# A mixed change to a tuned encoder layer: weight splits moved to VectorE, a norm moved to another buffer, row picks moved ahead of a weight split

## The chip, the core and the metric

The kernel runs on one core of a Trainium2 chip. The metric is the device time of one execution in microseconds (us). Matrix products run on TensorE (PE in the profile, its weight loads PEld), elementwise work on VectorE (DVE), activations and copies on ScalarE (ACT), and further elementwise work, indexed gathers and accumulating scatters on GpSimd (POOL). SyncE (SP) issues the plain transfers. Each engine takes its instructions in the order of its own queue; between engines semaphores hold them back.

## What is computed

One encoder layer, for 2048 sample tokens and 512 prompt tokens with the same weights, in float32:

```
h = x + W_out @ concat[DiffAttn(n), BandGQA(n)],  n = RMSNorm(x)
y = h + ExpertChoiceSwiGLU(RMSNorm(h))

def expert_choice_ffn(x, w_router, w_gate, w_up, w_down):     # once for each group
    C = CAPACITY_FACTOR * T // N_EXPERTS                       # 256 sample rows, 64 prompt rows
    aff = jax.nn.softmax(jnp.dot(xt, w_router), axis=-1)
    gates, idx = lax.top_k(aff.T, C)                           # each of 16 experts takes its C best tokens
    xe = xt[idx]
    h = jax.nn.silu(einsum('ecd,edf->ecf', xe, w_gate)) * einsum('ecd,edf->ecf', xe, w_up)
    ye = einsum('ecf,efd->ecd', h, w_down) * gates[..., None]
    y = zeros.at[idx].add(ye)
```

The model width is 1024 and each expert's inner width 1024.

## The kernel before, in words

Tokens are worked on in 20 blocks of 128 (b = 0 to 19; 16 of the sample, `NS`, and 4 of the prompt, `NP`; `NB` is 20). A float32 product is made of three faster ones (`mm3`, L167 to L169): each operand is split into a high part (a copy that rounds, on ScalarE) and a low part (the difference, on VectorE or GpSimd).

The stage that matters first is the loop over blocks that makes the output projection (`outproj`), adds the residual (L1409), and makes the second norm (`norm2`): ScalarE squares and sums a row into `dst`, GpSimd takes the power -1/2, and the norm `n2` is written (by VectorE at L1424, or, for blocks that `slow` names, by ScalarE and GpSimd) and stored to DRAM (`n2s_d` for the sample, `n2p_d` for the prompt). One block later the norm is transposed and split (`split_n`), multiplied with the router's weights (`router`, L1433) and turned into affinities (`router_2`: softmax; `router_3`: transposed copy for the search).

Work of one block is woven into the products of another by hand: `at(t, f, ...)` books a function for tick t of the current block, and `tick` is called after each product of eight. A generator does the top-k: `choose` finds each expert's threshold by ten steps of three bits. A step counts on VectorE (`flags`, L1204), asks TensorE for a sum over the candidates (L1212), and reads the answer (`r`, L1213). Each `yield` ends a slot. `first_sample` runs the sample's search over the last blocks' ticks (`SLOTS`), then writes the one-hot selections of expert 0 (`onehot_s`, L1308) and picks its rows.

`pick` turns one-hot selections into row numbers: small products on TensorE (L1329), a copy `ax` and `idx` and `gate` on VectorE (L1332 to L1334), then gathers on GpSimd (L1342), two of 128 sample rows and one of prompt rows.

After the last block `last_block`, another generator, makes the router of block 19, and, woven into expert 0's first product, the prompt's search and the picks for experts 0 and 1. Expert 0's first turns (`first_turn`, L1570) transpose the gathered rows.

The experts follow one after another. The first product (`gate_up`) goes over eight chunks f of the inner width; after half of a chunk it calls `mid`, which books the split of a later chunk's weights (`w_split`), loads (`w_load`) and, in certain chunks, the next expert's one-hots (f = 0) and pick, and from f = 4 on the transposes of the next expert's rows (`turn`, L1584). Experts 2 to 15 make the second product in blocks (`down_blocks`) and end with scatters (L1810) that add the rows to the output: `x.ys[1]`, the two halves of the prompt's `x.ys[2]` (both write `out_p`, so that the second waits until the first has landed), and `x.ys[0]`.

Weights of 1 MB a chunk are loaded into a ring of two `wraw` buffers, and every third early one into the room of `affsT` (the sample's transposed affinities, no longer needed once the search is over). In expert 0, `w_split` works by quarters of 512 columns: the high part on ScalarE (L1292) and the low part on GpSimd (L1293).

Of the kernel before, what the change touches and what calls it, by code (L numbers as in the profile page):

```python
# [8 lines left out]
F32 = mybir.dt.float32  # L9
# [9 lines left out]
P = 128  # L19
D = 1024  # L20
# [6 lines left out]
E = 16  # L27
# [80 lines left out]
def hybrid_encoder_kernel(tc, a, out_s, out_p):  # L108
# [11 lines left out]
    with ctx:  # L120
# [33 lines left out]
        def pow_mhalf(out, in_, n):  # L154
            nc.gpsimd.tensor_tensor(out, in_, nhalf[:, :n], op=OP.pow)
# [19 lines left out]
        with ExitStack() as st:  # L175
# [521 lines left out]
            def at(dt, f, *args):  # L697
                events.append((clock[0] + dt, len(events), f, args))
# [579 lines left out]
                raws.append((key, raw))  # L1278
                loaded[0] += 1

        def w_split(part=None):

            if raws:
                key, raw = raws[0]
                if not part:
                    split[key] = [wsp.tile([P, 2048], F32R, name=f"w{c}") for c in ("hi", "lo")]
                hi, lo = split[key]
                if part is None:
                    split_w(hi, lo, raw)
                else:  # L1290
                    cs = slice(part * 512, (part + 1) * 512)
                    nc.scalar.activation(hi[:, cs], raw[:, cs], AF.Copy)  # L1292
                    nc.gpsimd.tensor_sub(lo[:, cs], raw[:, cs], hi[:, cs].bitcast(F32))  # L1293
                if part is None or part == 3:
                    raws.pop(0)

# [63 lines left out]
        with ExitStack() as st:  # L1360
# [24 lines left out]
            def slow(b):  # L1385
                return NS <= b < NB - 1
# [21 lines left out]
                h = H[b]  # L1408
                nc.vector.tensor_add(h[:, cs], o, h[:, cs])  # L1409

            def norm2(b):
                out, n2d, r, aff = where(b)
                h = H[b]
                nc.sync.dma_start(out[r * P:(r + 1) * P, :], h)
                s = wk.tile([P, 3], F32, name="dst")
                n2 = tk.tile([P, D], F32, name="n2")
                nc.scalar.activation(n2, h, AF.Square, accum_out=s[:, 0:1])
                nc.vector.tensor_scalar(s[:, 1:2], s[:, 0:1], 1.0 / D, EPS, op0=OP.mult, op1=OP.add)
                pow_mhalf(s[:, 2:3], s[:, 1:2], 1)
                if slow(b):  # L1420
                    nc.scalar.activation(n2, h, AF.Copy, scale=s[:, 2:3])
                    nc.gpsimd.tensor_mul(n2, n2, ffn_g)
                else:
                    nc.vector.scalar_tensor_tensor(n2, h, s[:, 2:3], ffn_g, op0=OP.mult, op1=OP.mult)  # L1424
                nc.sync.dma_start(n2d[r * P:(r + 1) * P, :], n2)
                N2[b] = n2
# [40 lines left out]
                    split_wo_l(1, h, k, nc.vector)  # L1467
            split_w(wrh[:, :, 0, :], wrh[:, :, 1, :], wrr)

            SLOTS = (2, 7, 12, 17), (4, 9, 14), (1, 6, 11, 14, 16, 17)  # L1470
            gens = []

            def slot():
# [9 lines left out]
            for b in range(NB):  # L1483
                if b + 2 < NB:
                    MX[b + 2] = load_mx(b + 2)
                if b + 1 < NB:
                    load_res(b + 1)
                if b == 0:
                    for j in range(HEADS * NP):
                        at(14 + 18 * j, lambda j=j: Prompt(0, j // NP, j % NP).start())  # L1490
                    for h in range(2, HEADS):
                        at(72 * h - 50, load_prompt, h)
                if b == NS + 1:
                    rest.close()
                    wsp = pool(ctx, "wsE", 3, side="right")
                if b >= 1:
                    if slow(b - 1):
                        at(12, split_n, b - 1)
                    t = 15 if slow(b - 1) else 13
                    at(t, router, b - 1)  # L1500
                    at(t + 2, router_2, b - 1)
                    if b < NS:
                        at(t + 7, router_3, b - 1)
                    if b == NS:
                        gens.append(first_sample(X[0]))
                        parts = gate_parts(affs, auxs, NS, "s")
                        at(17, router_3, b - 1)
                        at(17, slot)
                if b > NS:
                    at(1, router_3, b - 2) if b > NS + 1 else None  # L1510
                    for t in SLOTS[b - NS - 1]:
                        at(t, slot)
                    at(9, next, parts, None)
                    at(14, next, parts, None)
                if b == 2:
                    at(3, places, auxs, NS)
                    at(9, places, auxp, NP)
                if NS < b < NB - 1:
                    for i in range(4):
                        at(1 + 4 * i, w_split, i)  # L1520
                if b == 0:
                    tick(8)
                else:
                    outproj(b, 0)
                if b >= 1 and not slow(b - 1):
                    split_n(b - 1)
                tick(1)
                if b + 1 < NB:
                    MT[b + 1] = split_m(MX[b + 1])
                tick(1)  # L1530
                outproj(b, 1)
                norm2(b)
                if b == 1:
                    w_load()
                    w_load()
            while gens:
                slot()

        stay.close()

# [6 lines left out]
        with ExitStack() as st:  # L1547
# [123 lines left out]
            def down_blocks(x):  # L1671
# [69 lines left out]
                p = bank("gu1")  # L1741
                product(p, 5, "22b")
                added(y[2][1], q, 2, y[2][1])
                scatter_p(x, x.ys[2])
                added(y[0][1], p, 0, y[0][1])
                scatter(x.idx[:, 0:1], x.ys[0], out_s)
                w_split()
                w_load()

# [64 lines left out]
                for gi in range(2):  # L1814
                    scatter(x.idx[:, gi:gi + 1], x.ys[gi], out_s)

            def scatter_p(x, y):
                for hf in range(2):
                    scatter(x.idx[:CP, 2:3], y[hf * CP:(hf + 1) * CP, :], out_p)

            def last_block(x, y):
# [55 lines left out]
            for f in range(FC):  # L1877
                for t in (3, 8, 13):
                    at(t, next, lb, None)
                for i in range(4):  # L1880
                    at(2 + 4 * i, w_split, i)
                at(15, w_load)
                gate_up(x, f, 2 * P, lambda: None, lambda: tick(1))
            for half in range(2):
# [6 lines left out]
            for e in range(1, E):  # L1891
# [10 lines left out]
                for f in range(FC):  # L1902
                    def mid():
                        if y is not None and f >= 4:
                            turn(y, 2 * (f - 4))
                        if e < 2:
                            w_split()
                            w_load()
                        else:
                            if f:  # L1910
                                split_sums(x, f - 1)
                            if f < 6:
                                w_split()
                            else:
                                split_block(x, ("11", "21")[f - 6])
                            if f < 4:
                                w_load()
                        if y is not None and f == 0:
                            onehot_s(y)
                            onehot_p(y)  # L1920
                        if y is not None and f == (1 if e > 2 else 2):
                            pick(y, 0, 3)
                            if e == 2:
                                scatter_p(X[0], X[0].yp)
# [69 lines left out]
```

## Time and profile before

| What | Value |
|---|---|
| median of three runs | 3185.86 us (3182.3 to 3187.32) |
| profiled execution | 3189.75 us, span 3188.0 us |
| TensorE busy | 3045.8 us, 96% of the span |
| VectorE busy | 2349.1 us, 74% |
| ScalarE busy | 1680.5 us, 53% |
| GpSimd busy | 1208.9 us, 38% |
| end of the output projection | 1705.39 us |
| expert 0's first product starts | 1725.96 us |
| a middle expert (3 to 14) | about 88 us |

Times of rows are microseconds from the start of the span. Busy time of TensorE is modelled, and its matmuls overlap; a row of the timeline gives the start, the duration, the engine, the line, the operation and its tiles, and in brackets how long the engine stood idle before it and what ended that.

### The profile page before, as it was taken

Reading aid. Unit: us, or ns where it says so; the run is one execution under the profiler, and the core shown is the slowest. Engines: PE = TensorE matmul, PEld = TensorE weight load, DVE = VectorE, ACT = ScalarE, POOL = GpSimd, SP = SyncE. Lnnn points to the kernel's source line nnn. Section 1 sums busy time; section 2 is a strip of 40 time slices with the busy share of each in tenths; the row PEclk is TensorE's granted clock in tenths of the full one; section 3 lists DMA queues with packets and bytes.
Section 4 is the critical chain, followed back from the end, with each engine's and each line's share of the span. In section 5 each row is a group of like instructions: output and inputs, shape, how many; then the busy total and the mean of one; then the engine's idle time right before and its main releaser. Section 6 shows DMA issues by size and latency. Waiting matters only on the chain. (4 is left out here: it accounts for less than half of the span.)

```text
span 3188.0 us, 50336 instructions
## 1 busy us (share of the span) xinstructions
PE 3045.8 (96%) x18996; PEld 2717.8 (85%) x18996; DVE 2349.1 (74%) x4297; ACT 1680.5 (53%) x3199; POOL 1208.9 (38%) x1116
## 2 busy tenths in 40 slices
PE   7998999998999999999997999999999999999997
PEld 5887888886888888888876899999999989999996
DVE  6887777777787788854566656778877767777876
ACT  4333666656777777743333454445555444444553
POOL 3665655554556556632234302122212122222211
PEclk9999999999999999999998999999999999999998
DMA  6664111136030301055533667665555556666553
GB/s 215 179 178 153 57 46 47 56 75 154 22 88 21 87 21 59 28 172 159 156 120 132 196 207 231 198 198 172 177 191 182 192 180 204 212 198 197 170 177 117
DMA packets 169138, 448.26 MB, mean 141 GB/s; under 512 B 15232, under 2 KB 91648, under 8 KB 138560
## 3 DMA queue, kind: packets, MB, share of 16 engines
q1 hardware_dynamic: 152608, 388.68, 37.4%
q0 software_dynamic: 16288, 56.37, 7.7%
q8 instruction: 150, 2.46, 0.3%
q14 instruction: 92, 0.75, 0.1%
HBM read 359.54 MB, written 82.84 MB: 139 GB/s over the span
## 5 line engine op out<-in xcount | busy, mean ns | idle before, releaser
L167 PE MATMUL gu<-xeh,whi 128*128 128x320 f32 (+1 forms) x2048 | 641.8, 313 | 0.0
L169 PE MATMUL gu<-xeh,wlo 128*128 128x320 f32 (+1 forms) x2048 | 631.0, 308 | 0.7 <-DVE wlo L161 0.7
L168 PE MATMUL gu<-xel,whi 128*128 128x320 f32 (+1 forms) x2048 | 630.7, 308 | 0.0
L161 DVE TENSOR_TENSOR wlo<-wraw,whi 128x2048 fp32r<-128x2048 f32 x180 | 412.8, 2296 | 163.5 <-ACT whi L160 163.5
L160 ACT ACTIVATE whi<-wraw 128x2048 fp32r<-128x2048 f32 x180 | 343.2, 1911 | 106.5 <-DMA wraw<-w_gu 50.4
L167 PEld LDWEIGHTS gu<-xeh,whi 128*128 128x128 f32 x2048 | 387.5, 189 | 2.9 <-issue 2.3
L168 PEld LDWEIGHTS gu<-xel,whi 128*128 128x128 f32 x2048 | 386.9, 189 | 0.6
L169 PEld LDWEIGHTS gu<-xeh,wlo 128*128 128x128 f32 x2048 | 386.1, 189 | 0.9 <-DVE wlo L161 0.9
L907 DVE TENSOR_REDUCE cmx<-s 128x1 f32<-128x1024 f32 x256 | 309.4, 1220 | 63.5 <-PE s L895 61.0
L1810 POOL DMA_INDIRECT out_dram<-y,idx x62 | 125.3, 2021 | 582.7 <-DVE y L1692 337.2
L918 ACT ACTIVATE p<-s,cmx 128x1024 f32<-128x1024 f32 x256 | 285.1, 1115 | 81.4 <-DVE cmx L909 78.0
L895 PE MATMUL s<-kd,qd 128*128 128x512 f32 x1024 | 295.3, 416 | 23.8 <-ACT p L918 22.2
L960 PE MATMUL cpo<-vd,aT 128*128 128x128 f32 x2048 | 267.3, 276 | 0.7 <-DVE co L965 0.7
L960 PEld LDWEIGHTS cpo<-vd,aT 128*128 128x128 f32 x2048 | 250.8, 192 | 8.8 <-ACT aT L953 4.6
L167 PE MATMUL z<-w,xh 128*128 128x512 f32 (+1 forms) x624 | 241.1, 386 | 11.7 <-ACT w L163 6.8
L940 POOL TENSOR_SCALAR p<-p,cr 128x1280 f32<-128x1280 f32 (+1 forms) x80 | 144.1, 1802 | 228.6 <-DVE cr L930 190.4
L169 PE MATMUL z<-w,xl 128*128 128x512 f32 (+1 forms) x624 | 229.8, 368 | 0.3 <-POOL xl L692 0.3
L895 PEld LDWEIGHTS s<-kd,qd 128*128 128x128 f32 x1024 | 177.9, 191 | 61.2 <-ACT p L918 35.6
L168 PE MATMUL z<-w,xh 128*128 128x512 f32 (+1 forms) x624 | 229.2, 367 | 0.5 <-DVE w L164 0.5
L953 ACT ACTIVATE aT<-cpt 128x512 f32<-128x512 f32 x272 | 161.8, 595 | 118.3 <-PE cpt L948 114.5
L1636 POOL TENSOR_TENSOR s<-hr,s 128x128 f32<-128x128 f32 x56 | 26.5, 474 | 486.8 <-DVE hr L1604 486.8
L942 POOL TENSOR_TENSOR p<-p,p 128x1280 f32<-128x1280 f32 (+1 forms) x80 | 207.3, 2591 | 6.6
(416 smaller groups left out, 7172.7 us busy)
## 6 DMA issues: line engine op xcount, KB each, us to landing
wraw<-w_gu SPq DMA_DIRECT2D x136, 1024.0 KB, 6.8
b<-w_dn SPq DMA_DIRECT2D x42, 1024.0 KB, 9.1
wraw<-w_dn SPq DMA_DIRECT2D x40, 1024.0 KB, 4.9
xr<-xT SPq DMA_DIRECT2D x40, 512.0 KB, 4.8
kd<-k_d SPq DMA_DIRECT2D x16, 1024.0 KB, 16.5
xtok<-x SPq DMA_DIRECT2D x20, 512.0 KB, 5.0
q_d<-hl SPq DMA_DIRECT2D x20, 512.0 KB, 3.5
k_d<-hl SPq DMA_DIRECT2D x20, 512.0 KB, 3.4
```

The source lines that it names most:

```text
L160: nc.scalar.activation(hi, raw, AF.Copy)
L161: nc.vector.tensor_sub(lo, raw, hi.bitcast(F32))
L167: nc.tensor.matmul(out, xh, wh, start=start, stop=False)
L168: nc.tensor.matmul(out, xh, wl, start=False, stop=False)
L169: nc.tensor.matmul(out, xl, wh, start=False, stop=stop)
L895: nc.tensor.matmul(s, q, u.keys(c, hl, k0), start=(hl == 0), stop=(hl == 1))
L907: nc.vector.tensor_reduce(m[:, j % 2:j % 2 + 1], u.S[j], axis=AX, op=OP.max)
L918: nc.scalar.activation(u.pr[c][:, half * 1024:(half + 1) * 1024], u.S.pop(j), AF.Exp, bias=u.mx[:, c, 2:], scale=SCALE, accum_out=u.sm[:, ...
L940: nc.gpsimd.tensor_scalar(p1, p1, u.r[:, 1:2], 1.0, op0=OP.mult, op1=OP.mult)
L942: nc.gpsimd.tensor_tensor(p0, p0, p1, op=OP.add)
L953: nc.scalar.activation(u.aT[:, 4 * g:4 * g + 4, :], u.pt, AF.Copy)
L960: nc.tensor.matmul(u.po, u.aT[:, kb, :], u.values(kb), start=(kb == 0), stop=(kb == u.nb - 1))
```

## The change

Three edits stand side by side. First, `w_split` gets an argument for the engine of the low part, and expert 0's first product passes VectorE; the quarters that are split in the block loop before it stay on GpSimd. Second, the last block's norm is written to the room of `affsT` (`n2l`), the router of block 18 is moved behind the block loop, and the end of `first_sample` (one-hots, then pick) is called right behind the last residual add and inside the last `norm2`, between the power and the norm. Third, from expert 3 on the pick for the next expert is called ahead of the weight split of chunk f = 1, and the last two scatters of the expert before it (the prompt's second half and `x.ys[0]`) are called behind that pick; experts 14 and 15 issue theirs at their own end, as before.

```diff
-        def w_split(part=None):
+        def w_split(part=None, eng=nc.gpsimd):
...
-                    nc.gpsimd.tensor_sub(lo[:, cs], raw[:, cs], hi[:, cs].bitcast(F32))
+                    eng.tensor_sub(lo[:, cs], raw[:, cs], hi[:, cs].bitcast(F32))
...
-            def norm2(b):
+            def norm2(b, mid=lambda: None):
...
-                n2 = tk.tile([P, D], F32, name="n2")
+                if b < NB - 1:
+                    n2 = tk.tile([P, D], F32, name="n2")
+                else:
+                    n2 = tk.tile([P, NS * P], F32, name="n2l", tag="affsT")[:, :D]
...
                 pow_mhalf(s[:, 2:3], s[:, 1:2], 1)
+                mid()
...
-            SLOTS = (2, 7, 12, 17), (4, 9, 14), (1, 6, 11, 14, 16, 17)
+            SLOTS = (2, 7, 12, 17), (4, 9, 14), (1, 6, 11, 14, 16)
...
-                if b >= 1:
+                if 1 <= b < NB - 1:
...
-                norm2(b)
+                if b == NB - 1:
+                    slot()
+                    norm2(b, lambda: list(gens and gens.pop(0)))
+                else:
+                    norm2(b)
...
+            split_n(NB - 2)
+            router(NB - 2)
+            router_2(NB - 2)
...
-                scatter_p(x, x.ys[2])
+                scatter_p(x, x.ys[2], (0,))
                 added(y[0][1], p, 0, y[0][1])
-                scatter(x.idx[:, 0:1], x.ys[0], out_s)
+                if x.e > E - 3:
+                    late_scatters(x)
...
+            def late_scatters(x):
+                scatter_p(x, x.ys[2], (1,))
+                scatter(x.idx[:, 0:1], x.ys[0], out_s)
+
-            def scatter_p(x, y):
-                for hf in range(2):
+            def scatter_p(x, y, halves=(0, 1)):
+                for hf in halves:
...
-                    at(2 + 4 * i, w_split, i)
+                    at(2 + 4 * i, w_split, i, nc.vector)
...
+                            if y is not None and f == 1 and e > 2:
+                                pick(y, 0, 3)
+                                late_scatters(X[e - 1])
                             if f < 6:
                                 w_split()
...
-                        if y is not None and f == (1 if e > 2 else 2):
+                        if y is not None and f == 2 and e <= 2:
                             pick(y, 0, 3)
```

The change shifts line numbers: L1409 stays, L1424 becomes L1428, L1433 becomes L1437, L1445 becomes L1449, L1609 becomes L1620, L1810 becomes L1822.

On VectorE, at the end of the last block, the program before had these rows (`slots` is the sample's search result, `wraw` holds expert 0's one-hots, `xres` is the residual sum, `lg`, `dsm`, `affp` and `many` belong to block 18's softmax):

```order
L1450 RECIPROCAL dsm<-dsm 128x1
L1451 TENSOR_SCALAR affp<-lg,dsm 128x16
L1453 TENSOR_SCALAR many<-lg,dsm 128x112
L1308 TENSOR_SCALAR wraw<-iota_s,slots 128x256 x16
L1409 TENSOR_TENSOR xres<-do,xres 128x512
L1418 TENSOR_SCALAR dst<-dst 128x1
L1424 SCALAR_TENSOR_TENSOR n_17775<-xres,dst,ffn_g 128x1024
L1332 COPY ax<-s 128x10
L1333 SCALAR_TENSOR_TENSOR idx<-ax 128x2
```

And the changed program has these at the same place:

```order
L1237 SCALAR_TENSOR_TENSOR slots<-sels 128x256
L1409 TENSOR_TENSOR xres<-do,xres 128x512
L1308 TENSOR_SCALAR wraw<-iota_s,slots 128x256 x16
L1421 TENSOR_SCALAR dst<-dst 128x1
L1332 COPY ax<-s 128x10
L1333 SCALAR_TENSOR_TENSOR idx<-ax 128x2
L1334 TENSOR_REDUCE gate<-ax 128x2
L1428 SCALAR_TENSOR_TENSOR n2l<-xres,dst,ffn_g 128x1024
L161 TENSOR_TENSOR ntl<-dpt,nth 128x1024
L1449 COPY lg<-cpo 128x16
```

The residual add has moved ahead of the one-hots, the index ahead of the norm, and block 18's split (`ntl`) and softmax behind both.

On VectorE in a middle chunk of expert 0's first product (`hr`, `hl`: activation and its low part; `rp` to `gep`: one step of the prompt's search), the changed program has the four `wlo` rows that stood on GpSimd before:

```order
L1620 TENSOR_TENSOR hl<-hr,hh 128x256
L1293 TENSOR_TENSOR wlo<-wraw_17918,whi 128x512
L1213 CAST rp<-cnt 112x1
L1202 TENSOR_SCALAR candp<-basep,rp 112x1
L1204 TENSOR_SCALAR flags,cnp<-affpT,candp 112x512
L1206 TENSOR_SCALAR thp<-thp,rp 112x1
L1208 TENSOR_SCALAR basep<-thp,steps 112x1
L1209 TENSOR_SCALAR gep<-cnp 112x1
L1293 TENSOR_TENSOR wlo<-wraw_17918,whi 128x512
L1213 CAST rp<-cnt 112x1
```

Each search step now follows a `wlo` in VectorE's queue; the other rows keep their order.

On GpSimd, from expert 2's end into expert 3's chunk f = 1, the program before had the four scatters (`out_dram<-y`) and then the three gathers (`xe`) for expert 4:

```order
L1810 DMA out_dram<-y_20658,idx 2048x1024
L1810 DMA out_dram<-y_20659,idx 512x1024 x2
L1810 DMA out_dram<-y_20657,idx 2048x1024
L1342 DMA xe_21011<-n2s_d,idx 128x1024
L1342 DMA xe_21013<-n2s_d,idx 128x1024
L1342 DMA xe_21015<-n2p_d,idx 128x1024
```

The changed program:

```order
L1822 DMA out_dram<-y_20658,idx 2048x1024
L1822 DMA out_dram<-y_20659,idx 512x1024
L1342 DMA xe_21003<-n2s_d,idx 128x1024
L1342 DMA xe_21005<-n2s_d,idx 128x1024
L1342 DMA xe_21007<-n2p_d,idx 128x1024
L1822 DMA out_dram<-y_20659,idx 512x1024
L1822 DMA out_dram<-y_20657,idx 2048x1024
```

The gathers have moved ahead of the last two scatters.

## Rows read from the trace of the kernel before

**Rows 1.** TensorE's waits, 2030 to 3188 us: total us, times, longest.

```profile
PE pt L1584 <- DMA xe<-n2p_d,idx: 17.9, 12, 3.6
PE pt L1584 <- DMA xe<-n2s_d,idx: 1.5, 1, 1.5
```

**Rows 2.** Waits of TensorE and its weight loads in one stage, 2560 to 2648 us.

```profile
PE pt L1584 <- DMA xe<-n2p_d,idx: 3.6, 1, 3.6
...
PEld pt L1584 <- DMA xe<-n2s_d,idx: 1.8, 1, 1.8
```

**Rows 3.** Timeline of GpSimd in expert 6, start and duration in us.

```profile
2301.48 1.44 POOL L1810 DMA_INDIRECT out_dram<-y,idx  x1 [7.23 <-DMA out_dram<-y,idx]
...
2306.45 0.99 POOL L1342 DMA_INDIRECT xe<-n2s_d,idx  x1 [0.30 <-issue]
```

**Rows 4.** Timeline of VectorE in the same stage.

```profile
2302.42 2.29 DVE L161 TENSOR_TENSOR wlo<-wraw,whi 128x2048 fp32r<-128x2048 f32 x1 [1.52 <-ACT whi L160]
...
2304.83 0.16 DVE L1333 SCALAR_TENSOR_TENSOR idx<-ax 128x3 int32<-128x3 f32 x1
```

**Rows 5.** Timeline of TensorE in the same stage.

```profile
2299.86 0.24 PE L1329 MATMUL cnt<-auxp,ohp 128*128 128x5 bf16 x4
...
2322.29 0.33 PE L1584 MATMUL pt<-ident,xe 128*128 128x128 f32 x1 [0.74 <-DMA xe<-n2p_d,idx]
```

**Rows 6.** Same stage: ScalarE's timeline; a stretch's busy times, clock, DMA share, GB/s.

```profile
2312.28 1.92 ACT L160 ACTIVATE whi<-wraw 128x2048 fp32r<-128x2048 f32 x1 [0.23 <-DMA wraw<-w_gu]
...
2316.00:2320.00 4.00, 4.00 (x30) 4.00 (x28) 1.64 (x5) 0.66 (x3) 0.00 (x0) 1.00 1.03 415
```

**Rows 7.** Timeline of TensorE from the last block to expert 0.

```profile
1696.70 1.03 PE L1392 MATMUL dpt<-ident,n 128*128 128x128 f32 x8
...
1700.25 0.64 PE L1433 MATMUL cpo<-ntl,wrh 128*32 128x128 f32 x8
...
1704.26 0.24 PE L1442 MATMUL cpo<-ident,lt 32*128 32x32 f32 x1
...
1705.00 0.39 PE L169 MATMUL do<-wo,mtl 128*128 128x512 f32 x1
...
1713.85 1.97 PE L1828 MATMUL pt<-ident,n 128*128 128x128 f32 x8 [3.35 <-DVE n L1424]
...
1717.53 1.05 PE L1433 MATMUL pt<-xel,wrh 128*32 128x128 f32 x8
...
1722.85 3.46 PE L1570 MATMUL pt<-ident,wraw 128*128 128x128 f32 x15 [0.80 <-DMA wraw<-n2s_d,idx]
```

**Rows 8.** Timeline of VectorE at the same place.

```profile
1706.37 0.32 DVE L1453 TENSOR_SCALAR many<-lg,dsm 128x112 f32<-128x112 f32 x1
1706.61 3.22 DVE L1308 TENSOR_SCALAR wraw<-iota_s,slots 128x256 bf16<-128x256 bf16 x16
1709.74 0.68 DVE L1409 TENSOR_TENSOR xres<-do,xres 128x512 f32<-128x512 f32 x1
```

**Rows 9.** Timeline of GpSimd at the same place: expert 0's gathers.

```profile
1714.35 1.11 POOL L1342 DMA_INDIRECT wraw<-n2s_d,idx  x1 [1.88 <-DVE fold L1867]
1715.77 0.97 POOL L1342 DMA_INDIRECT wraw<-n2s_d,idx  x1 [0.31 <-issue]
```

**Rows 10.** Timeline of TensorE in expert 0: search answers, and a pick's products.

```profile
1743.85 0.16 PE L1212 MATMUL cnt<-gep,same 112*112 112x1 bf16 x1 [0.37 <-DVE gep L1209]
...
1750.44 0.16 PE L1212 MATMUL cnt<-gep,same 112*112 112x1 bf16 x1 [0.37 <-DVE gep L1209]
...
1768.60 0.94 PE L1329 MATMUL cnt<-auxs,oh 128*128 128x5 bf16 x32 [1.13 <-DVE ax L1332]
```

**Rows 11.** VectorE's groups by form, 1640 to 1720 us: count, busy us, mean ns.

```profile
L161 DVE TENSOR_TENSOR mtl<-cpt,mth 128x512 fp32r<-128x512 f32 x3 | 2.0, 680 | 0.0
```

**Rows 12.** Timeline of VectorE in expert 0: the prompt's one-hots, twice.

```profile
1762.50 2.84 DVE L1313 TENSOR_SCALAR ohp<-iota_p,slotp 128x128 bf16<-128x128 bf16 x4
...
1768.72 0.73 DVE L1313 TENSOR_SCALAR ohp<-iota_p,slotp 128x128 bf16<-128x128 bf16 x4
```

**Rows 13.** GpSimd's groups by form, 1725 to 1790 us: count, busy us, mean ns.

```profile
L1293 POOL TENSOR_TENSOR wlo<-wraw,whi 128x512 fp32r<-128x512 f32 x32 | 40.6, 1297 | 18.0 <-ACT whi L1292 17.9
```

## The prediction

> **What bounds the kernel now.** I read the share of busy time first: TensorE is busy 96% of the span, so a change pays only where TensorE stands still, or where it makes TensorE stand still. Next, the waits of TensorE over the last twelve experts but the very last one (experts 3 to 14) [rows 1]: there are two rows and no others. The transposes of the next expert's rows (`turn`) wait for the gather of these rows, 17.9 + 1.5 = 19.4 us over twelve stages of some 88 us. One stage holds 3.6 + 1.5 = 5.1 of it (the single wait for a sample gather is there too, as the row of its weight load shows [rows 2]); the other eleven have 14.3, or 1.3 each.
>
> Then one ordinary stage, engine by engine. GpSimd's queue [rows 3] holds two accumulating scatters of the expert before, the first of which stands 7.23 us on an earlier scatter's landing, and only behind them the first of three gathers, at 2306.45. The index that it needs is written by VectorE at 2304.83 [rows 4], behind a weight split that itself had waited 1.52 us for ScalarE. TensorE had finished the selecting products at 2299.86 + 0.24 = 2300.10, and stands before the missing rows until 2322.29 [rows 5]. So the gather is late by its issue: by the two scatters and by the split, not by the selection.
>
> The second place is the seam between the last token block and expert 0 [rows 7 to 9]: the last product of the output projection ends at 1705.39, the first gathered rows are transposed at 1722.85, and between them TensorE does little. The third is expert 0's first product, where VectorE carries the prompt's threshold search and GpSimd the low parts of the weights [rows 10 to 13].
>
> **Experts 3 to 14: the pick ahead of the split, the scatters behind the gathers.** Nothing is added; four things change place. VectorE's copy and index can start when TensorE has the selecting products (2300.10) and VectorE is free (2302.42 - 1.52 = 2300.90 [rows 4]); with some 0.2 us each the index is there at about 2301.3 and the first gather starts at about 2301.5 instead of 2306.45: 4.9 us earlier. GpSimd is free then, because the scatter that stood there until 2301.48 now comes after. The new wait is VectorE's copy on TensorE's products; queued behind it is the weight split, which has to wait for ScalarE until 2302.42 anyway, so it costs nothing (without that cover it would cost 0.4 us of VectorE, two products ahead of the use). The scatters go out at about 2306, when the earlier ones have landed, so their 7.23 us wait goes nowhere; their tiles are written again only by the down products at the stage's end. A lead of 4.9 us covers a wait of 1.3 us, and nearly all of the long one. What is late next in the stage is nothing that the rows of TensorE show, so I take the whole: **-19.4** against the profiled execution, and 12 x 1.3 = **-15.6** against an execution without the long stage. Bounds: half of it, if the gather lands only half as much earlier (its transfer took the DMA engines' share from the weight loads); not more than 19.4.
>
> A rule of the Trainium skill speaks against the earlier gather (SBUF — State Buffer, the section "SBUF: two separate sides", its box on a DMA blocked by VectorE): while VectorE holds the port pair in its fast two-port modes, GpSimd can't write the descriptors of its DMAs. By it a gather could stand behind one VectorE instruction, 2.29 us for the longest here [rows 4], which would leave a lead of 2.6 us and the same sum but for some 2 us of the long stage; no run here shows it yet.
>
> **The seam.** Block 18's transposes, router products and softmax leave the end of block 19. On TensorE that is 1.03 + 2 x 0.64 + 0.24, less overlap some 2.3 us [rows 7], so the projection ends at about 1703.1 instead of 1705.39. VectorE no longer runs the softmax ahead of the one-hots (it ended at 1706.37 + 0.32 [rows 8]); it adds the residual first (0.68) and then writes the one-hots (3.13, from 1706.61 to 1709.74): they end at about 1707.0. ScalarE's square and GpSimd's power run beside and right behind them. Then come copy and index, no longer behind the residual, the square, the power and the norm: the first gather starts at about 1708.2 instead of 1714.35 [rows 9]. Its partner took from 1715.77 to before 1722.85 to land, 7.05 us, so the rows are there at about 1716.7.
>
> But the moved work now stands between. TensorE transposes block 18's norm from about 1707.5. From there to the second half of the router products the rows have 3.55 us (1696.70 to 1700.25); here TensorE runs at its slower row (eight transposes in 1.97 us instead of 1.03), so 0.9 more: 1712.0, plus 1.05 for that half. The small transpose follows at 1713.5, and the softmax ends 2.43 us later (1704.26 to 1706.69), at 1715.9. The last norm's transposes up to the end of its router products take 4.73 us by rows (1713.85 to 1718.58), from 1713.8: 1718.5, plus 0.4 for the transposed softmax that must pass in between: 1718.9. That is later than the landing, so the chain and no longer the gather sets the end. Sixteen transposes at 0.23 us end at 1722.6; they now end at 1722.85 + 3.46 = 1726.31: **-3.7**. Bounds: -6.0 if only the landing counts, -1.5 if two of the handovers cost a microsecond more each. The other room for the last norm takes no time of its own; it is what lets block 18's norm still be read when block 19's square is written.
>
> **Expert 0's first product.** Thirty-two subtractions of 512 columns leave GpSimd (1.297 us each [rows 13]) for VectorE; the nearest row has 0.68 us for one, some 0.60 from start to start [rows 11]. TensorE's steps of the search stand 6.60 us apart, and 0.37 us of that is a wait for VectorE (1743.85 to 1750.44 [rows 10]): VectorE is already the later one there. Per chunk of columns, two of the four subtractions lie between a count and its answer from TensorE, where half of each is hidden (0.3 each), and two beside the activation's product, in full (0.58 each): +1.75. The search fills chunks 1 to 3; chunk 1 gains back what it lost, since `hl` no longer meets GpSimd: +3.5 for the three. Chunk 4 I take as even. In chunk 5 TensorE waits 1.13 us for VectorE's copy behind the one-hots [rows 10]; ahead of it come two subtractions (+1.2), and the prompt's one-hots fall from 2.84 us to the 0.73 us that the same four take a little later, when GpSimd is still [rows 12]: -0.8. From chunk 6 on VectorE has room. With 0.4 us less wait at the first transposes of the down product: **+2.3**. Bounds: -1, if the answers hide more; +13.6, if the 20 subtractions of chunks 1 to 5 lie on the path at 0.68 each with nothing back.
>
> The Trainium skill has a rule for the stretched one-hots (SBUF — State Buffer, Who interferes with whom): VectorE in a two-port mode, or with two inputs in SBUF, and GpSimd shut each other out for a whole instruction. The trace agrees, 2.84 against 0.73 [rows 12]. Without it this term would be 2.1 us dearer, and the sum 3171 instead of 3169.
>
> **The sum.** Against the profiled execution (3189.75 us, span 3188.0): -19.4 - 3.7 + 2.3 = 3168.95. Against the median of the three runs, 3185.86, from which the profiled one differs by 3.9, about what its one long stage has over the others (5.1 - 1.3 = 3.8): -15.6 - 3.7 + 2.3 = 3168.9. I predict **3169**.
>
> **Rivals.**
> *VectorE becomes the bound of expert 0.* For it: TensorE already waits for VectorE at each search step [rows 10]. Against it: from chunk 4 on GpSimd's interference goes. With +13.6 instead of +2.3: 3185.86 - 15.6 - 3.7 + 13.6 = 3180.2; halfway, 3174.5.
> *The gathers land no earlier,* since the DMA engines, not the issue, set the landing: the change does not do what it says. For it: from the first issue to the last landing lie some 15.8 us [rows 3, 5], twice the 8.5 us of the two gathers in the seam (1714.35 to 1722.85), so the engines are shared with the weight loads. Against it: two scatters stood ahead in the same queue, and now don't. All waits stay: 3184.5; half: 3176.7.
> *Slower: the weight loads slip.* The gathers now run while the weights of chunk 5 come in, whose split had to wait 0.23 us for its load [rows 6]; that load is just in time. The split ends some 4.2 us after 2312.28, and TensorE uses it in chunk 5, at about 2326 (half a chunk's products behind 2322.29): 9 us of room, where the three gathers' 1.5 MB at the 415 GB/s of a full stretch [rows 6] are 3.6 us. It decides at a slip of 11 us a stage: 12 x 2 = 24 us lost against 17 won, 3193.
>
> **Chances.** Forecast (3163 to 3174): 0.70. VectorE dearer in expert 0 (3174 to 3180): 0.12. Gathers no or half earlier (3176 to 3185): 0.10. Better than forecast, the seam limited by the landing and the outlier's like in more runs (3157 to 3163): 0.04. Loads slip: 0.04. A difference under 0.2%, 6.4 us, can hardly be told from none. Faster (below 3179.5): 0.70 + 0.04 and most of the two dearer cases, 0.88; within: 0.08; slower: 0.04. The range 3161 to 3179 leaves out the slip, most of the unmoved gathers and the ends: under 2 in 10.
>
> **What would show it.** Experts 3 to 14: the first gather about 2 us behind the selecting products, both scatters after the third gather, no wait of `turn` for a gather in TensorE's list. Seam: one-hots at once behind the last residual add, first gather some 6 us earlier, and TensorE coming to the gathered rows after they have landed. Expert 0: no GpSimd subtraction, search steps 8.3 us apart in chunks 2 and 3, one-hots of the prompt at 0.73. It is wrong if `turn` still waits, if the steps lie over 9 us apart, or if the chain of block 18's router takes over 12 us from the one-hots on.

## The result, and the profile after

The changed kernel takes 3162.48 us (median of four runs) beside 3186.59 of the kernel before: 0.9928 of it, 95% interval 0.9911 to 0.9945. Run again in a later comparison it was 0.9942 (0.9926 to 0.9957). The time lies 6.5 us under the forecast of 3169: inside the range of 3161 to 3179, but 0.5 us outside the band of 3163 to 3174 that had the chance of 0.70, in the case that was given 0.04. Two of the reasons behind the forecast do not hold.

The profiled execution took 3165.03 us, span 3163.2, 24.8 less than before. The parts, by the same marks in both traces: eleven stages from expert 3's one-hots on (2029.61 to 3005.42 before, 2028.59 to 2981.52 after) -22.9; the seam from the residual add of block 19's first half (1695.79, after 1695.65) to the end of the gathered rows' transposes -4.6; expert 0's first product +5.2; its second product and the two experts behind it -1.5 (granted clock 0.98 in 1785 to 1945 us before, 0.99 after); the rest -1.0.

**An ordinary stage after.** The list of TensorE's waits from 1990 to 3170 us is empty where [rows 1] had two rows. Its weight loads' waits in the same stretch, before (first fence) and after (second): who waited, us in total, times, longest.

```profile
PEld pt L1584 <- DMA xe<-n2p_d,idx: 20.7, 12, 3.8
PEld pt L1584 <- DVE xel L1586: 1.8, 10, 0.2
PEld pt L1584 <- DMA xe<-n2s_d,idx: 1.8, 1, 1.8
```

```profile
PEld pt L1595 <- DVE xel L1597: 2.2, 12, 0.2
```

22.5 us of waiting for gathers are gone. 21.4 of them lay in the eleven stages, which became 22.9 shorter, and 1.0 in the stretch behind them. The row of the matmuls, 19.4 for all twelve waits, from which the prediction took its size, is the smaller of the two. GpSimd, then VectorE and TensorE in expert 6 after, as [rows 3, 4, 5]:

```profile
2282.95 1.56 POOL L1822 DMA_INDIRECT out_dram<-y,idx  x1 [24.13 <-DVE y L1703]
2284.82 2.66 POOL L1822 DMA_INDIRECT out_dram<-y,idx  x1 [0.31 <-issue]
2295.18 1.01 POOL L1342 DMA_INDIRECT xe<-n2s_d,idx  x1 [7.70 <-issue]
2296.49 0.97 POOL L1342 DMA_INDIRECT xe<-n2s_d,idx  x1 [0.31 <-issue]
2297.77 1.86 POOL L1342 DMA_INDIRECT xe<-n2p_d,idx  x1 [0.30 <-issue]
2299.94 1.49 POOL L1822 DMA_INDIRECT out_dram<-y,idx  x1 [0.30 <-issue]
```

```profile
2294.23 0.17 DVE L1333 SCALAR_TENSOR_TENSOR idx<-ax 128x3 int32<-128x3 f32 x1
...
2296.47 2.35 DVE L161 TENSOR_TENSOR wlo<-wraw,whi 128x2048 fp32r<-128x2048 f32 x1 [2.01 <-ACT whi L160]
```

```profile
2293.13 0.24 PE L1329 MATMUL cnt<-auxp,ohp 128*128 128x5 bf16 x4
```

The index is written ahead of the split, the first gather starts 1.8 us behind the selecting products, and the scatter's 7.23 us wait is gone, all as forecast. But another view moved more. Issues of transfers, 1990 to 3170 us (count, median us from issue to landing), before and after:

```profile
out_dram<-y,idx POOLq DMA_INDIRECT x54, 6.4
xe<-n2s_d,idx POOLq DMA_INDIRECT x24, 12.2
xe<-n2p_d,idx POOLq DMA_INDIRECT x12, 13.4
```

```profile
out_dram<-y,idx POOLq DMA_INDIRECT x56, 9.6
xe<-n2s_d,idx POOLq DMA_INDIRECT x24, 5.1
xe<-n2p_d,idx POOLq DMA_INDIRECT x12, 8.5
```

A sample gather lands 5.1 us behind its issue instead of 12.2. (The scatters themselves now land later, 9.6 instead of 6.4, and no wait of TensorE shows it.) Counted from the stage's one-hots, in expert 6, the first gather was issued at 10.8 and landed, by the median, at 23.0 (2306.45 - 2295.63, + 12.2); now 6.3 and 11.4. Of 11.6 us, 4.5 come from the issue and 7.1 from a shorter way.

**The seam.** TensorE, as [rows 7]; VectorE, as [rows 8]; GpSimd, as [rows 9]:

```profile
1702.57 0.40 PE L169 MATMUL do<-wo,mtl 128*128 128x512 f32 x1
1707.32 1.91 PE L1392 MATMUL dpt<-ident,n 128*128 128x128 f32 x8
1710.34 1.06 PE L1437 MATMUL cpo<-nth,wrh 128*32 128x128 f32 x8 [1.11 <-ACT nth L160]
1711.60 1.06 PE L1437 MATMUL cpo<-ntl,wrh 128*32 128x128 f32 x8 [0.20 <-DVE ntl L161]
1713.02 0.31 PE L1446 MATMUL cpo<-ident,lt 32*128 32x32 f32 x1 [0.36 <-ACT lt L1440]
1713.26 1.97 PE L1844 MATMUL pt<-ident,n2l 128*128 128x128 f32 x8
...
1717.07 1.05 PE L1437 MATMUL pt<-xel,wrh 128*32 128x128 f32 x8
1717.92 0.41 PE L1581 MATMUL pt<-ident,wraw 128*128 128x128 f32 x1
1718.60 3.02 PE L1581 MATMUL pt<-ident,wraw 128*128 128x128 f32 x15 [0.26 <-DMA wraw<-n2s_d,idx]
```

```profile
1703.00 0.69 DVE L1409 TENSOR_TENSOR xres<-do,xres 128x512 f32<-128x512 f32 x1 [0.18 <-PE do L169]
1703.61 3.21 DVE L1308 TENSOR_SCALAR wraw<-iota_s,slots 128x256 bf16<-128x256 bf16 x16
```

```profile
1708.14 1.96 POOL L1342 DMA_INDIRECT wraw<-n2s_d,idx  x1 [0.63 <-DVE gate L1334]
1710.41 0.97 POOL L1342 DMA_INDIRECT wraw<-n2s_d,idx  x1 [0.31 <-issue]
```

The projection ends at 1703.0 (forecast 1703.1), the first gather starts at 1708.14 (1708.2), and router chain and landing now end together: the transposes wait 0.26 us for the rows.

**Expert 0's first product.** TensorE's search answers after, and the pick's products, as [rows 10]:

```profile
1737.20 0.17 PE L1212 MATMUL cnt<-gep,same 112*112 112x1 bf16 x1
1741.25 0.16 PE L1212 MATMUL cnt<-gep,same 112*112 112x1 bf16 x1 [1.98 <-DVE gep L1209]
1744.42 0.20 PE L1212 MATMUL cnt<-gep,same 112*112 112x1 bf16 x1
1746.91 0.17 PE L1212 MATMUL cnt<-gep,same 112*112 112x1 bf16 x1
1750.56 0.16 PE L1212 MATMUL cnt<-gep,same 112*112 112x1 bf16 x1 [1.58 <-DVE gep L1209]
...
1767.72 0.94 PE L1329 MATMUL cnt<-auxs,oh 128*128 128x5 bf16 x32 [1.73 <-DVE ax L1332]
```

VectorE by form, 1720 to 1790 us, as [rows 13], and the prompt's one-hots, as [rows 12]:

```profile
L1293 DVE TENSOR_TENSOR wlo<-wraw,whi 128x512 fp32r<-128x512 f32 x32 | 21.6, 685 | 1.4 <-ACT whi L1292 0.7
```

```profile
1763.13 0.74 DVE L1313 TENSOR_SCALAR ohp<-iota_p,slotp 128x128 bf16<-128x128 bf16 x4
```

The whole product as one stretch, before and after (stretch, length, busy us of PE, PEld, DVE, ACT, POOL, then granted clock, DMA share, GB/s):

```profile
1726.31:1783.29 56.98, 51.68 (x451) 50.12 (x450) 41.27 (x131) 25.22 (x54) 42.46 (x38) 0.99 0.54 187
```

```profile
1721.62:1783.75 62.13, 54.36 (x452) 52.76 (x450) 49.57 (x167) 25.41 (x55) 7.13 (x9) 0.95 0.51 179
```

It grew by 5.15 us, in two about equal parts: TensorE stands 7.8 us instead of 5.3, and is busy for 54.4 us instead of 51.7 with the same matmuls, because the granted clock fell. The clock in two stretches of 4 us after (before, every such stretch from 1728 to 1792 us shows 1.00):

```profile
1740.00:1744.00 4.00, 2.75 (x15) 2.75 (x15) 3.79 (x14) 0.76 (x2) 0.00 (x0) 0.69 0.45 188
...
1768.00:1772.00 4.00, 4.00 (x44) 4.00 (x41) 2.94 (x11) 0.89 (x3) 2.79 (x3) 0.60 0.29 61
```

Each fall, to a mean of 0.6 to 0.7 over 4 us (between the levels of 2.4 and 1.2 GHz), comes right behind a stand of TensorE: the 1.98 us that end at 1741.25, and the 1.73 us, for VectorE's `ax`, that end at 1767.72. Behind the stand of 1.58 us that ends at 1750.56 there is none.

### The profile page after: what moved, and what is told of

Its sections match the earlier page's. It is cut to its first block, busy times and chain, and to the rows that moved or that the text cites. A ratio compares the mean times of both kernels' runs of the same rounds, so it can differ in the third digit from the quotient of the medians.

```text
span 3163.2 us, 50333 instructions
## 1 busy us (share of the span) xinstructions
PE 3045.8 (96%) x18996; PEld 2719.2 (86%) x18996; DVE 2355.5 (74%) x4329; ACT 1680.4 (53%) x3199; POOL 1168.5 (37%) x1084
## 5 line engine op out<-in xcount | busy, mean ns | idle before, releaser
L1822 POOL DMA_INDIRECT out_dram<-y,idx x62 | 119.7, 1931 | 490.4 <-DVE y L1703 337.2
L167 PE MATMUL z<-w,xh 128*128 128x512 f32 (+1 forms) x624 | 241.2, 387 | 10.9 <-ACT w L163 6.7
```

What stands on the lines that cost most here:

```text
L167: nc.tensor.matmul(out, xh, wh, start=start, stop=False)
```

## The experiments

Each ratio is to the kernel before on the same chip, whose medians there were 3181.6 to 3184.7 us. "First product" is the stretch above with its granted clock; "landing" is the median for sample and prompt gathers, 1990 to 3170 us (a dash: the profile gives none); "`turn`" is TensorE's total wait for gathers there.

| run | median us | ratio (95%) | first product, clock | landing | `turn` |
|---|---|---|---|---|---|
| before, first profile | | | 57.0, 0.99 | 12.2 / 13.4 | 19.4 |
| e1_experts | 3165.77 | 0.9950 (0.9931 to 0.9969) | 57.2, 0.99 | 5.2 / 9.0 | none |
| e2_low_gpsimd | 3160.69 | 0.9936 (0.9917 to 0.9955) | 57.7, 0.97 | 5.2 / 7.4 | none |
| e3_seam | 3176.73 | 0.9982 (0.9966 to 0.9997) | 56.3, 1.00 | 11.0 / 12.8 | 13.5 |
| e4_low_vector | 3185.10 | 1.0012 (0.9998 to 1.0026) | 60.5, 0.96 | 11.9 / 13.1 | 11.1 |
| e5_pick_only | 3181.34 | 0.9995 (0.9984 to 1.0006) | 56.8, 1.00 | 12.3 / 10.7 | 9.6 |
| e6_scatters_only | 3165.30 | 0.9943 (0.9928 to 0.9959) | 57.0, 0.99 | - | none |
| e7_after_again | 3164.06 | 0.9942 (0.9926 to 0.9957) | 61.9, 0.94 | - | none |
| e8_low_late | 3159.23 | 0.9928 (0.9913 to 0.9943) | 54.8, 1.00 | - | none |
| e9_swap | 3160.78 | 0.9934 (0.9920 to 0.9947) | 56.9, 1.00 | 7.4 / 10.4 | none |
| e10_half_front | 3166.29 | 0.9948 (0.9935 to 0.9961) | 57.2, 0.99 | 6.2 / 10.1 | none |
| e11_quarter3 | 3165.07 | 0.9944 (0.9931 to 0.9957) | 61.5, 0.97 | 5.4 / 7.7 | none |
| e12_swap_all | 3156.34 | 0.9919 (0.9902 to 0.9937) | 55.9, 0.97 | 7.5 / 10.4 | none |

**The three edits apart.** e1, e3 and e4 are the kernel before with one edit each (third, second, first in the order of the change section); e2 is the changed kernel without the first (from its edit, the line that decides):

```diff
...
-                    at(2 + 4 * i, w_split, i, nc.vector)
+                    at(2 + 4 * i, w_split, i)
```

> The kernel before with the third edit alone: from expert 3 on, pick ahead of the weight split and two scatters behind the gathers. If the whole gain of experts 3 to 14 comes from the earlier gathers, -15.6 us by the waits of TensorE in the kernel before (3171 us beside 3186.6), or -18 by the stage lengths of the changed kernel (some 86.4 us instead of 88.0); TensorE shows no wait of turn for a gather. Rival, that the stages became shorter by something that the other two edits brought: under 6 us gained, 3181 or more.

> The changed kernel, but expert 0's low parts go back to GpSimd; seam and experts as changed. If the move to VectorE costs what its profile shows (first product 62.1 us instead of 57.0, about 1 of it a dip of the clock), 3 to 5 us faster than the changed kernel, 3157.5 to 3159.5 us. If the prediction's +2.3 was right and the rest is that run's clock, 3160. Rival, the move to VectorE gains (the one-hots and the activation's low part no longer stand behind GpSimd): 3163 or slower.

> The kernel before with the seam edit alone (last norm in the room of affsT, block 18's router behind the loop, one-hots and pick early). By the prediction -3.7, by the profile of the changed kernel -4.7: 3182 to 3183 us beside 3186.6, the first transposes of gathered rows end at 1721.5 to 1722.6 instead of 1726.3. Rival, that what is won at the seam is lost again in expert 0, whose first chunks then meet the search or the weights later: 3186, within 1 us of before.

> The kernel before with expert 0's low parts on VectorE, nothing else. By the prediction +2.3 (3189), by the profile of the changed kernel +4 to +5 (3191 us): search steps 8.3 to 9.3 us apart in chunks 2 and 3 instead of 6.6, one-hots of the prompt at 0.73 us. Rival, that the answers hide the subtractions: 3185.6, steps within 7 us.

At 3181.6 us, e1 gains 0.50%, 15.9 us, with stages of 86.2 to 87.2 us and no wait of `turn`. e3 gains 0.18%, 5.7 us with an interval from 1 to 11; in its trace the seam, from the same add (1694.90) to the transposes' end (1720.61), takes 25.7 us, against 30.5 before, 30.7 in e1 and 30.2 in e4: 4.8 us won, and its first product, 56.3, gives none of it back. e4 costs 0.12%, with an interval that just reaches no change; its first product is 3.5 us longer than before's. e2's is 4.4 shorter than the changed kernel's. By this stretch the move of the low parts to VectorE loses in both surroundings; in the total time neither difference is clear of the noise (e2's 0.9936 lies between the two ratios of the changed kernel, 0.9928 and 0.9942).

**Which half of the third edit works.** e5 has the pick ahead of the split, with the scatters at their old place; e6 the scatters behind the pick, with the pick at its old place:

```diff
+                            if y is not None and f == 1 and e > 2:
+                                pick(y, 0, 3)
                             if f < 6:
...
-                        if y is not None and f == (1 if e > 2 else 2):
+                        if y is not None and f == 2 and e <= 2:
```

```diff
...
                             pick(y, 0, 3)
+                            if e > 2:
+                                late_scatters(X[e - 1])
```

> The kernel before with half of the third edit: the pick stands ahead of the weight split, but both scatters stay in front of the gathers. In expert 6 of the kernel before, the scatters leave GpSimd at 2306.15 and the index is written at 2304.99, so with the index early the scatters alone set the first gather. If the issue behind the scatters sets the landing, the gathers start no earlier than before and nothing is gained: within 2 us of before, TensorE's waits of turn in experts 3 to 14 stay at 13 to 20 us. Rival, that what counts is VectorE's order (the index, or the split's place in the stage): half or more of what the whole edit gave, 8 us or more gained.

> The other half: both scatters behind the gathers, the pick still behind the weight split. The index (2304.99 in the rows) then sets the first gather, at some 2305.8 with the 0.8 us that the changed kernel shows between the two, instead of 2306.45: 0.7 us earlier. If the landing follows the issue one to one, each stage keeps 0.6 or more of its 1.3 us wait: 6 to 10 us gained, 3174 or more where before is 3182. Rival, that the scatters' own traffic is what delayed the gathers: all of it gained, -16 to -18, no wait of turn left.

The pick ahead of the split gives nothing (0.9995), the scatters behind the gathers give all of it (0.9943, as the changed kernel's 0.9942 in the same comparison), though the gathers start only 0.67 us earlier in the stage. e6, GpSimd:

```profile
2299.94 1.00 POOL L1342 DMA_INDIRECT xe<-n2s_d,idx  x1 [11.45 <-issue]
```

Counted from the one-hots of its stage (2289.79) that is 10.15 us, where before had 10.82 and e5 11.35. Over all twelve stages the median is 11.2 us before, 11.2 in e5, 10.7 in e6 and 6.3 after. An earlier issue is therefore not what the gain comes from; what was put into GpSimd's queue just ahead is. The rival in e6's expectation was right, not the theory. e5 missed in one point: its `turn` waits 9.6 us, less than the 13 to 20 expected, and yet no time was gained that can be told.

**Which scatter.** e9 changes the order of two scatters in the kernel before, and nothing else; e10 leaves the prompt's second half in front of the gathers and puts only `x.ys[0]` behind them:

```diff
-                scatter_p(x, x.ys[2])
+                scatter_p(x, x.ys[2], (0,))
                 added(y[0][1], p, 0, y[0][1])
                 scatter(x.idx[:, 0:1], x.ys[0], out_s)
+                scatter_p(x, x.ys[2], (1,))
...
```

> The kernel before with one swap: the scatter of x.ys[0] goes out ahead of the prompt's second half instead of behind it, so that it uses the 7 us in which GpSimd stood for the first half's landing; all four scatters still stand in front of the gathers, the pick still behind the split. The index sets the first gather (0.7 to 1 us earlier than before), and only the small scatter goes out close ahead of it. If the gathers' landing (12.2 us behind the issue in the kernel before, 5.1 in the changed one) is held by the transfers put into the queue just ahead of them, it falls to 6 to 9 us and 9 to 18 us are gained. Rival, that any scatter in front costs the whole: landing stays at 11 to 12 us, within 4 us of before.

> The prompt's second half stays in front of the gathers at its old place, x.ys[0] goes behind them; the pick stays behind the split. Same issue of the gathers as with both scatters behind (index at some 2305 in expert 6's rows, gather 0.8 later). If the bytes just ahead hold the landing, it is like the swap's, 6 to 9 us, and 9 to 18 us are gained; if the large scatter's traffic matters wherever it goes, less than half of that. Rival, that only GpSimd's issue counts: 0.7 us a stage, 6 to 10 us gained, landing unchanged at 12 us.

Either is enough: 0.9934 and 0.9948, and no wait of `turn`. The landing of the sample's gathers, in e9 and then in e10:

```profile
xe<-n2s_d,idx POOLq DMA_INDIRECT x24, 7.4
```

```profile
xe<-n2s_d,idx POOLq DMA_INDIRECT x24, 6.2
```

GpSimd in e9, expert 6:

```profile
2290.29 1.55 POOL L1811 DMA_INDIRECT out_dram<-y,idx  x1 [2.43 <-DVE oh L1308]
2295.82 1.42 POOL L1811 DMA_INDIRECT out_dram<-y,idx  x1 [3.97 <-DMA out_dram<-y,idx]
2300.05 1.00 POOL L1342 DMA_INDIRECT xe<-n2s_d,idx  x1 [2.81 <-issue]
```

The large scatter goes out in the time in which GpSimd had stood still, and the gather behind it is issued 10.7 us behind the one-hots (2289.34), 0.1 us earlier than before; over the twelve stages the median is 10.9 beside 11.2. That is less than the 0.7 to 1 us expected, while the gain, 0.66% of 3183.3 or 21 us (17 to 25), reached above the 9 to 18. So with the issue all but unmoved and all scatters still ahead, an `x.ys[0]` that has gone out 9.8 us before the gather, instead of 3.2 (2303.23 and 2306.45), takes the wait away.

**The clock and the low parts.** e7 is the changed kernel again; e8 gives the low parts to GpSimd up to the first quarter of chunk 4; e11 only the fourth quarter in chunks 0 to 3:

```diff
-                    at(2 + 4 * i, w_split, i, nc.vector)
+                    at(2 + 4 * i, w_split, i, nc.vector if 4 * f + i > 16 else nc.gpsimd)
```

```diff
+                    at(2 + 4 * i, w_split, i, nc.gpsimd if i == 3 and f < 4 else nc.vector)
```

> The changed kernel once more, beside the others on one chip. 0.9928 to 0.995 of before; in expert 0's first product (from the end of the first transposes to the first down product) 60.0 us if the granted clock does not fall there, some 1.5 us more for each fall. If the 62.1 of the earlier profile belongs to the move to VectorE itself, 62 again at full clock.

> The changed kernel, with expert 0's low parts on GpSimd up to the first quarter of chunk 4, on VectorE from there on. If the price of the move lies in the search steps of chunks 2 and 3 (+1.9 each) and its gain at the end (-0.9 at gteqp in chunk 4, -0.7 at the prompt's one-hots in chunk 5), the first product takes 55 us at full clock, 5 less than the changed kernel's 60 and 1.5 less than with all on GpSimd; 0.1% to 0.15% faster than the changed kernel. Rival, that a fall of the clock or the weights take it back: 57 or more, no difference to the changed kernel that can be told.

> The changed kernel, but in chunks 0 to 3 of expert 0 the fourth quarter's low part goes back to GpSimd, so that no two subtractions stand between one count and the next. The step that stood 1.98 us on VectorE then stands 1.2 to 1.4 us. If the falls of the granted clock behind that step come from TensorE's long stand, they go with it, at least the one between the search and the one-hots: first product 58 us instead of 62. If the falls have nothing to do with the stand, only the two steps' 0.6 us each go: 60.5 to 61 us, clock 0.94 as before in that stretch.

e7 has two falls again (0.67 in 1752 to 1756 us, 0.57 in 1768 to 1772) and 61.9 us, so the 62.1 was not one execution's accident. e8 meets its 55:

```profile
1723.85:1778.62 54.77, 50.85 (x450) 49.75 (x450) 41.35 (x150) 25.34 (x55) 27.64 (x26) 1.00 0.59 204
```

TensorE stands 3.9 us of it, 1.4 less than before. In the total time e8's 0.9928 and e7's 0.9942 have overlapping intervals. e11 misses 58: the search's stand is cut in two (0.67 and 1.39 us, about the same sum), so its steps stay 8.45 us apart. Its search ran at full clock, but TensorE's stands add up to 8.4 us instead of 7.8, and a fall behind the `ax` wait stayed.

**A better one.** e12 has the seam as changed, e8's split and e9's swap in place of the third edit:

> The seam as changed, expert 0's low parts on GpSimd up to the first quarter of chunk 4 and on VectorE from there on, and in place of the whole third edit only the swap of the two scatters. If the parts add up (seam -4.7, end of expert 0's first product -2, swap -18 to -21), 0.9915 to 0.993 of before, 3156 to 3161 us, no wait of turn in TensorE's list, the first product 55 us. Rival, that the earlier seam moves the stages against each other so that the swap alone no longer covers the gathers: waits of turn come back, 3163 or more.

It is the fastest of all, 0.9919; against the changed kernel's 0.9942 and e8's 0.9928, from another comparison, the intervals overlap. Its first product is 55.9 instead of 55: one fall of the clock behind the `ax` wait. Its first gathers start 11.25 us behind the one-hots by the median, beside 11.21 before, and TensorE waits for none of them.

## Why the prediction was right in time and partly wrong in reason

**Experts 3 to 14: the size about right, the step wrong.** -15.6 was forecast against the median, and e1 alone gives -15.9 (interval -22 to -10); against the profiled execution -19.4 was forecast and the stages show -22.9, since the fitting row was that of the weight loads, 22.5 in all. The step that failed is "the gather is late by its issue: by the two scatters and by the split" and the lead of 4.9 us built on it. The order of index and split had no part that can be told: an index ahead of the split gains nothing (e5), one behind it loses nothing (e6). Of the two scatters what counts is not that they hold up the issue, but that the large one goes out close ahead of the gathers: moving it away takes the wait out with the issue nearly as it was (e9). The rival of the landing set by the DMA engines saw the 15.8 us between first issue and last landing, and drew the wrong end from it: that the change would then do nothing. The size came out because it was read from the waits themselves, which vanish whichever way the gathers come earlier. The row that would have told was the landing time of 12.2 us in the list of issues, beside some 7 us in the seam, where no scatter stands ahead; I put the difference down to the weight loads, but they are still there in e9, where it is 7.4 us.

Why a scatter close ahead lengthens the landing, the runs don't show. The Trainium skill (DMA: Bandwidth & Descriptors, Queues, rings and completion order) states, in a paragraph on the queues of SP and ACT, that a DMA engine takes one ring's descriptors in order, and that the write of a semaphore lands only after every earlier write of that engine, across its queues; by it a gather would report only behind the scatter's writes. The landings agree (12.2 with the large scatter 3.2 us ahead, 7.4 and 6.2 with the small one, 5.1 without), but waiting in the ring, waiting for the writes and plain sharing of the DMA engines with the scatter's traffic were not told apart.

The 13.5 and 11.1 us of `turn` in e3 and e4, whose experts are as before, beside 19.4 in the first profile, suggest that this term is not the same in each execution; the kernel before was profiled only once.

**The seam: right, 1.0 us too small.** -3.7 was forecast, 4.6 to 4.8 were measured. The transposes of the gathered rows began at 1717.92 instead of 1718.9: the small transpose stood at 1713.02 instead of 1713.5, and the 0.4 us added for the transposed softmax were already inside the 4.73 us of the rows they were added to, as this row of the kernel before tells:

```profile
1715.61 0.42 PE L1459 MATMUL pt<-ident,many 128*112 128x128 f32 x1
```

What was to set the end, the chain or the landing, came out as nearly a tie.

**Expert 0's first product: the stands right, the clock left out.** +2.3 was forecast; the product grew by 5.15, and 4.95 in e7. The stands carry 2.5 of it, close to the working: search steps 8.45 us apart in e7 and e11 (8.3 forecast; the 9.31 from 1741.25 to 1750.56 above has a fall of the clock in it), the one-hots of the prompt at 0.74. Chunk 4 was not even, as assumed: a wait of 1.1 us for `gteqp` there is gone. What the sum put at nothing is the granted clock: 54.4 - 51.7 = 2.7 us more of the same matmuls. Behind the search's 1.98 us stands it fell once in each of the three kernels that have them (after, e4, e7), that is behind three of five such stands; behind e11's 1.39 us not, nor in the search of any kernel with the low parts on GpSimd. Behind the `ax` wait it fell in four of six kernels with a stand of 1.7 us and in one of the others (e2, 1.13 us), so a stand of this size makes a fall likely, not certain; what decides it stays open. Of the edit, the part at chunk 4's end and after is a gain, the part over the search a loss (e8).

**The sum.** The forecast was 16.9 us below the median; the two comparisons give 22.9 (17.5 to 28) and 18.5 (14 to 24). Between the two profiled executions -20.8 was forecast and -24.7 came: the experts gave 4.4 more than their term (22.9 in eleven stages and 0.9 behind them, where the twelfth wait was), the seam gave 0.9 more, expert 0 took 2.9 more, and 1.6 were gained in stretches for which the prediction had no term, 1.5 of it behind expert 0's first product, whose cause stays open. So the errors of seam and expert 0 partly cancel, and that the total fell into the range is in part luck.

## What to carry to other kernels

Ahead of a gather, look in the list of issues at its time from issue to landing, not only at when it is issued: here a large scatter on the same queue a few microseconds ahead cost the whole wait, where a reordering of the index alone gained nothing, and it fitted into an earlier idle time of the queue. When elementwise work is moved onto an engine that TensorE waits for, count beside the stands what TensorE's clock may lose behind them. Move such work only where the receiving engine has room: here from the search's end on, not over it.

## What the hardware showed unexpectedly

A gather that begins while a weight split runs on VectorE is stretched until the split is over. In the fourteen traces, from 1960 us on, 166 of some 500 gathers begin more than 0.05 us inside a split of 2048 columns. Each ends 0.80 to 0.90 us behind the split and takes 1.5 to 3.05 us. None of the others takes more than 1.04 us, not even the six that begin within 0.04 us of a split's start (2296.49 after). e5, GpSimd and VectorE:

```profile
2299.33 1.00 POOL L1342 DMA_INDIRECT xe<-n2s_d,idx  x1 [0.30 <-issue]
2300.63 3.02 POOL L1342 DMA_INDIRECT xe<-n2s_d,idx  x1 [0.30 <-issue]
2303.95 0.94 POOL L1342 DMA_INDIRECT xe<-n2p_d,idx  x1 [0.30 <-issue]
```

```profile
2300.52 2.29 DVE L161 TENSOR_TENSOR wlo<-wraw,whi 128x2048 fp32r<-128x2048 f32 x1 [1.52 <-ACT whi L160]
```

2300.52 + 2.29 = 2302.81, and the gather, 3.02 instead of 0.97 us long, ends at 2303.65. It cost nothing after, since the rows now land with time to spare. In the kernel before, the prompt's gather, for which `turn` mostly waited, was stretched too (2.07 us at 2309.02); that alone does not make the wait, since in e9 it was stretched to 2.73 us and nothing waited.

The prediction weighed a rule on VectorE's two-port modes, and put the split of 2.29 us under it without showing that a split runs in such a mode. The same section of the Trainium skill (SBUF — State Buffer, SBUF: two separate sides) also states that a VectorE operation with two SBUF inputs and a GpSimd operation that reads SBUF share a port pair, and that whichever starts first has it for its whole instruction while the other blocks. The traces agree in part. The gather waits, as by that rule, up to 2 us; but a split that begins inside a gather does not (in e1 one at 2293.38, behind a gather's start at 2292.93, took the usual 2.29 us). Which of the two rules is at work, the runs don't tell.
